# A decoder block's MLP down projection: the right-hand column blocks take three feature pairs as block products instead of two

## The chip, the cores and the metric

The kernel runs on one NeuronCore of a Trainium2 chip. The metric is the device time of one execution in microseconds (us). The engines are named as in the profile: PE does the matmuls (PEld its weight loads), DVE works on vectors, ACT evaluates activations and copies, POOL is little used, and SP's queue issues most of the DMAs.

## The reference, cut to what matters

The reference is one decoder block on 256 tokens of width 2048 in float32: an input projection, a gated convolution branch and an attention branch, a mixing product, a layer norm, a squared-ReLU MLP beside a gated per-layer embedding, and a second layer norm. The change touches the MLP's second product alone.

```python
h = jnp.square(jax.nn.relu(x @ w_mlp_up[i])) @ w_mlp_down[i]     # (256,2048) (2048,8192) -> (256,8192) (8192,2048) -> (256,2048)
ple = (p[i] @ w_ple[i]) * jax.nn.sigmoid(x @ w_ple_gate[i])
x = _layer_norm(DN_ALPHA * x + h + ple, ln2_g[i], ln2_b[i])
```

## The kernel before, in words

**Precision.** Every float32 operand is split into a rounded part `hi` and a remainder `lo` (`split`, L67; for streamed weights `wchunk`, L77: a DMA into `raw`, an ACT copy into `whi` at L86, a DVE subtraction into `wlo` at L88). One product is then three matmuls: high by high, low by high, high by low.

**Chunks.** The MLP runs in four chunks `c` of 2048 hidden features (L1078). In a chunk, eight `up` calls (L1045) compute 256 features each, into `h` with the features on the partitions; their results leave PSUM through the ACT copies into `ab` (L1051), a tile with tag `m2` that has two buffers. Then the chunk's part of the down projection is added to `y`, whose 2048 columns are four blocks of 512. Chunks 0 to 2 do this in the way described here; chunk 3 has a form of its own (L1172 on) that the change leaves alone.

**Two ways for a product.** The direct way is `xstat` (L131, lines 144, 145 and 148 of the trace): for each tile of 128 features and each half of the tokens three matmuls of 512 columns. The other way is class `Seven` (L638): two feature tiles (a pair), two token halves and two column blocks form a 2x2 by 2x2 block product that takes seven block products instead of eight. Sums of the activation blocks (`sums_to`, L629) and sums of the weight blocks are multiplied instead of the blocks themselves. For a pair `p` the steps are

- `load`: 1 MB of weights by SP's queue (L650) into `rs` or into the upper half of the tile `tr`;
- `b_forms`: split of two weight blocks (one ACT and one DVE instruction on 128x1024) into `forms` 8 to 11 or 12 to 15;
- `t_sums`: three DVE instructions (L659, L661, L662) that write four weight sums into `tf`, the lower half of `tr`;
- `t_forms`: their split (ACT and DVE on 128x2048) into `forms` 0 to 7;
- `products`: six of the products, three matmuls each (L685), numbered 1, 3, 5, 7, 6, 4, each into its own PSUM accumulator;
- `second`: the seventh product (L697), with weights streamed by `wchunk`.

`close` (L1097) adds the accumulators to four quarters of `y`: one ACT copy and ten DVE instructions (L1107), by way of three sums u2, u3 and u4.

**A chunk's down part.** The first two column blocks take all eight pairs as block products (`sv`), woven into the `up` calls: pair `p - 2`'s products stand ahead of steps of `up` call `p`. The third and the fourth block (`third`, L1126, and `fourth`, L1149) do twelve of their sixteen feature tiles directly, and pairs 6 and 7 as block products of a second object (`sv2`, L1124). `sv2` reuses the activation sums of `sv`, adds three of its products onto the direct blocks' accumulators (`onto`, L1147), and ends with a close of its own (L1169). Its order by hand stands in L1127 to L1169: the steps of `third` and `fourth`, the seventh products of `sv` (`more`), and between them the preparation of the pairs. PSUM bank 4 holds first `sv`'s seventh product and then `sv2`'s product 6. The next chunk's first `up` call writes banks 0 and 3, its second banks 1 and 2, later ones 0 and 1 (L1074).

**What sets the order.** The program is written as one sequence, and the framework makes each engine's own order from it ahead of the run with a planner that simulates the timeline (L1287). An instruction whose operands the planner thinks ready can go ahead of earlier ones on its engine; `after(...)` pins some behind others. On the chip each engine then runs its list in that order. A tile with a tag is a buffer that the next tile of the same tag takes over when all uses of the old one are done: `tr` (tag O), `forms` (tag C) and `h` (tag B) have one buffer, so a new chunk's `tr` begins when the last use of the old one has ended.

## Time and profile before

| what | value |
|---|---|
| median of 3 runs | 1806.29 us (1803.21 to 1806.33) |
| the profiled execution | 1808.8 us, its span 1807.0 us |
| mean granted TensorE clock | 0.996 |
| PE busy | 1791.2 us, 9259 matmuls |
| DVE busy | 1424.9 us |
| ACT busy | 1014.5 us |
| read from HBM | 363.33 MB |

Busy time of PE counts pipelined matmuls, so it says that PE had work, not that it was at its peak. Where the text speaks of a wait, the profile names the instruction that stood and the one whose end released it. The clock column gives the share of full speed that was granted to TensorE in a stretch.

### The profile page before, as it was taken

How to read it: one execution, taken by the hardware profiler on the slowest of the kernel's cores; microseconds unless marked ns; L12 is line 12 of the kernel's file. 1: busy time of each engine (PE TensorE's matmuls, PEld its weight loads, DVE VectorE, ACT ScalarE, POOL GpSimd, SP SyncE). 2: the span in 40 equal slices, each digit the busy share in tenths (PEclk: the TensorE clock that was granted, in tenths of full speed). 3: DMA queues.
4: the chain of work that ended last, by engine and by line, in shares of the span. 5: the costliest groups of instructions: out<-in, count | busy, mean ns of one | idle time of the engine just before them, and what ended most of it. 6: DMA issues, size and time to landing. Idle time of an engine off the chain costs nothing.

```text
span 1807.0 us, 24866 instructions
## 1 busy us (share of the span) xinstructions
PE 1791.2 (99%) x9259; PEld 1532.3 (85%) x9259; DVE 1424.9 (79%) x2033; ACT 1014.5 (56%) x1344; POOL 18.5 (1%) x33
## 2 busy tenths in 40 slices
PE   9999999999999999999999999999999999999998
PEld 7889888888888888888888888888888888888886
DVE  6776776767787987897698678888888888889765
ACT  5555555555555555555454745765666466647561
POOL 1000000000000000000000000000000000000010
PEclk9999999999999999999999999999999999999999
DMA  8777665566655755865674567665766667666572
GB/s 262 223 237 215 178 176 164 166 183 175 175 164 175 235 200 191 272 210 178 202 271 163 194 230 252 214 206 189 244 200 213 197 206 223 202 213 197 186 275 74
DMA packets 255032, 367.07 MB, mean 203 GB/s; under 512 B 10773, under 2 KB 175477, under 8 KB 254400
## 3 DMA queue, kind: packets, MB, share of 16 engines
q1 hardware_dynamic: 250128, 354.07, 61.8%
q0 software_dynamic: 2112, 8.81, 1.4%
q10 hardware_dynamic: 2672, 2.62, 0.5%
q8 instruction: 72, 1.18, 0.3%
q14 instruction: 48, 0.39, 0.1%
HBM read 363.33 MB, written 2.12 MB: 202 GB/s over the span
## 4 chain that ended last, share of the span: by engine, by line
PE 95%; DVE 2%; DMA 1%; ACT 1%; issue 1%; SPq 0%; DVEq 0%; ACTq 0%
PE mm L106 16%; PE s L106 13%; PE s L685 12%; PE s L144 10%; PE s L145 10%; PE s L148 10%; PE mm L112 8%; PE s L112 6%; PE s L697 2%; PE s L1224 1%; PE sc L500 1%; PE mm L144 1%; PE mm L145 1%; PE mm L148 1%; PE po L350 1%
## 5 line engine op out<-in xcount | busy, mean ns | idle before, releaser
L86 ACT ACTIVATE whi<-raw 128x1024 fp32r<-128x1024 f32 (+2 forms) x567 | 588.7, 1042 | 501.4 <-PE s L145 185.2
L88 DVE TENSOR_TENSOR wlo<-raw,whi 128x1024 fp32r<-128x1024 f32 (+2 forms) x567 | 675.6, 1199 | 211.7 <-issue 52.5
L106 PE MATMUL mm<-xT,whi 128*128 128x512 f32 x1280 | 313.5, 393 | 0.1
L106 PE MATMUL s<-x,whi 128*128 128x512 f32 x1024 | 268.9, 395 | 6.1 <-ACT ab L1051 6.1
L106 PEld LDWEIGHTS mm<-xT,whi 128*128 128x128 f32 x1280 | 234.0, 189 | 44.8 <-issue 0.6
L106 PEld LDWEIGHTS s<-x,whi 128*128 128x128 f32 x1024 | 185.9, 191 | 39.3 <-ACT ab L1051 6.7
L112 PE MATMUL mm<-xT,wlo 128*128 128x256 f32 x1280 | 181.5, 285 | 0.0
L112 PEld LDWEIGHTS mm<-xT,wlo 128*128 128x128 f32 x1280 | 169.9, 190 | 7.5
L112 PEld LDWEIGHTS s<-x,wlo 128*128 128x128 f32 x1024 | 142.7, 192 | 12.2 <-DVE wlo L88 1.0
L112 PE MATMUL s<-x,wlo 128*128 128x256 f32 x1024 | 146.9, 284 | 0.0
L69 DVE TENSOR_TENSOR forms<-tr,forms 128x2048 fp32r<-128x2048 f32 (+1 forms) x63 | 112.9, 1796 | 24.5 <-ACT forms L68 22.9
L68 ACT ACTIVATE forms<-tr 128x2048 fp32r<-128x2048 f32 (+1 forms) x63 | 95.1, 1515 | 20.3 <-PE s L685 6.3
L685 PE MATMUL s<-forms,sums 128*128 128x512 f32 x408 | 106.1, 390 | 0.0
L685 PEld LDWEIGHTS s<-forms,sums 128*128 128x128 f32 x408 | 76.3, 188 | 16.0
L145 PE MATMUL s<-whi,h 128*128 128x512 f32 x208 | 80.9, 389 | 0.0
L144 PE MATMUL s<-whi,h 128*128 128x512 f32 x208 | 80.4, 389 | 0.0
L1051 ACT ACTIVATE ab<-s 128x512 f32<-128x512 f32 x64 | 37.7, 597 | 49.5 <-PE s L106 46.7
L148 PE MATMUL s<-wlo,h 128*128 128x512 f32 x208 | 65.0, 390 | 0.4 <-DVE wlo L88 0.4
L685 PE MATMUL s<-forms,h 128*128 128x512 f32 x204 | 60.9, 391 | 0.0
L685 PE MATMUL s<-forms 128*128 128x512 f32 x240 | 60.3, 389 | 0.0
L685 PEld LDWEIGHTS s<-forms 128*128 128x128 f32 x240 | 45.0, 188 | 9.3
L69 DVE TENSOR_TENSOR forms<-t,forms 128x1024 fp32r<-128x1024 f32 x40 | 48.5, 1220 | 3.0 <-ACT forms L68 2.7
(337 smaller groups left out, 2775.3 us busy)
## 6 DMA issues: line engine op xcount, KB each, us to landing
raw<-in_w_in_dram SPq DMA_DIRECT2D x204, 512.0 KB, 4.2
raw<-in_w_mlp_up_dram SPq DMA_DIRECT2D x128, 512.0 KB, 4.5
raw<-in_w_mlp_down_dram SPq DMA_DIRECT2D x69, 512.0 KB, 3.6
rs<-in_w_mlp_down_dram SPq DMA_DIRECT2D x17, 1024.0 KB, 7.0
tr<-in_w_mlp_down_dram SPq DMA_DIRECT2D x17, 1024.0 KB, 6.8
raw<-in_w_conv_out_dram SPq DMA_DIRECT2D x32, 512.0 KB, 4.4
raw<-in_w_attn_out_dram SPq DMA_DIRECT2D x32, 512.0 KB, 4.3
raw<-in_w_ple_gate_dram SPq DMA_DIRECT2D x32, 512.0 KB, 4.1
```

Source lines behind the costliest of these rows:

```text
L68: last_hi[0] = nc.scalar.activation(hi, src, AF.Copy).ins
L69: last_lo[0] = nc.vector.tensor_sub(lo, src, f32(hi)).ins
L86: last_whi[0] = nc.scalar.activation(hi, raw, AF.Copy).ins
L88: last_wlo[0] = nc.vector.tensor_sub(lo, raw, f32(hi)).ins
L106: last_mm[0] = nc.tensor.matmul(ps[f].rearrange("p a t -> p (a t)"), hi[:, kk, f * P:(f + 1) * P], mov[:, k0 + kk].rearrange("p a t -> p ( ...
L112: last_mm[0] = nc.tensor.matmul(ps[f][:, 1, :], lo[:, kk, f * P:(f + 1) * P], mov[:, k0 + kk, 0, :], start=False, stop=False, skip_group_c ...
L144: nc.tensor.matmul(ps[t], sta[:, kt0 + kt, 0, ts], hi[:, kk, :], start=(kt == 0), stop=False)
L145: nc.tensor.matmul(ps[t], sta[:, kt0 + kt, 1, ts], hi[:, kk, :], start=False, stop=False)
L148: last_mm[0] = nc.tensor.matmul(ps[t], sta[:, kt0 + kt, 0, ts], lo[:, kk, :], start=False, stop=(kt == nkt - 1)).ins
L685: last_mm[0] = nc.tensor.matmul(self.acc[n], first[:, a, :], self.forms[:, w, :], start=(p == self.p0 and i == 0 and n not in self.onto), ...
L697: last_mm[0] = nc.tensor.matmul(ps, self.mat[:, 2 * (q + k) + 1, a, 0:P], w[:, k, :], start=(own is not None and q + k == 0 and i == 0), s ...
L1051: nc.scalar.activation(ab[:, f], ps[f], AF.Copy)
```

## The change

In chunks 0 to 2 the third and fourth block take pairs 5, 6 and 7 as block products and the first ten feature tiles directly.

- `third` and `fourth` run 10 tiles (five steps) instead of 12 (six steps).
- `sv2` starts at pair 5. It multiplies pair 6 first (`first`, which starts the accumulators), then 5, then 7. By the turns 6: 0, 5: 1, 7: 2 the loads go to `rs`, `tr`, `rs`, and the block splits to `forms` 8, 12, 8.
- Pair 5's activation sums must last to the chunk's end; they move to the buffer with tag `pT` (L1058).
- `second` handles an odd number of pairs: 5 and 6 together, then 7 alone.
- In `third`, all products of pair 7 of `sv` stand ahead of the fourth step, where they stood in two parts before the fifth step; the first close follows one step earlier.
- The second close keeps u2, u3 and u4 in `tf`, the weight sums' tile, and no longer in two `m2` buffers.

```diff
--- before.py
+++ after.py
@@ -642,7 +642,7 @@
         def __init__(self, rows, c0, mat, raw, t, forms, b, t0, n=8, p0=0):
             self.rows, self.c0, self.mat, self.raw, self.t, self.forms, self.b, self.t0, self.n, self.p0 = (
                 rows, c0, mat, raw, t, forms, b, t0, n, p0)
-            self.raws, self.ts, self.sums, self.acc, self.onto = {}, {}, {}, {}, {}
+            self.raws, self.ts, self.sums, self.acc, self.onto, self.first = {}, {}, {}, {}, {}, p0
 
         def load(self, p):
             self.raws[p] = self.raw(p)
@@ -676,14 +676,14 @@
                          self.sums[p][:, {5: 0, 7: 1, 6: 2, 3: 3}[n]])
                 hi = {1: b, 3: b + 1, 5: t0, 7: t0 + 1, 6: t0 + 2, 4: t0 + 3}[n]
                 lo = hi + (2 if n in (1, 3) else 4)
-                if p == self.p0:
+                if p == self.first:
                     if n in self.onto:
                         self.acc[n] = self.onto[n]
                     elif n not in self.acc:
                         self.acc[n] = bank({1: 2, 3: 3, 5: 4, 7: 5, 6: 6, 4: 7}[n])
                 for i, (a, w) in enumerate(((0, hi), (1, hi), (0, lo))):
                     last_mm[0] = nc.tensor.matmul(self.acc[n], first[:, a, :], self.forms[:, w, :],
-                                                  start=(p == self.p0 and i == 0 and n not in self.onto),
+                                                  start=(p == self.first and i == 0 and n not in self.onto),
                                                   stop=(p == self.n - 1 and i == 2),
                                                   skip_group_check=n in self.onto).ins
 
@@ -691,8 +691,9 @@
 
             for q in range(self.p0, self.n, 2):
                 ps = self.onto.get(2) or (self.acc[1] if own is None else own)
-                hi, lo = wchunk(self.rows[:, q:q + 2, 1, self.c0:self.c0 + 512], 2, 512)
-                for k in range(2):
+                nk = min(2, self.n - q)
+                hi, lo = wchunk(self.rows[:, q:q + nk, 1, self.c0:self.c0 + 512], nk, 512)
+                for k in range(nk):
                     for i, (a, w) in enumerate(((0, hi), (1, hi), (0, lo))):
                         last_mm[0] = nc.tensor.matmul(ps, self.mat[:, 2 * (q + k) + 1, a, 0:P], w[:, k, :],
                                                       start=(own is not None and q + k == 0 and i == 0),
@@ -1055,7 +1056,10 @@
         nc.scalar.activation(m, m, AF.Square)
         split(m, h[:, 2 * p:2 * p + 2, 0, :], h[:, 2 * p:2 * p + 2, 1, :])
         if p < sv.n:
-            sv.sums[p] = post.tile([P, 4, 2, P], F32R, tag="sg", name="sums")
+            if p == 5 and c < 3:
+                sv.sums[p] = post.tile([P, 4, 2, P], F32R, tag="pT", name="sums", bufs=1)
+            else:
+                sv.sums[p] = post.tile([P, 4, 2, P], F32R, tag="sg", name="sums")
             sums_to(m, sv.sums[p])
 
     def down(c, j, banks, nkt=KT):
@@ -1094,9 +1098,8 @@
         def quarters(c0):
             return [y[:, t, a:a + 512] for t in range(2) for a in (c0, c0 + 512)]
 
-        def close(a, y00, y01, y10, y11):
-            u = [post.tile([P, 2, 512], F32, tag="m2", name="u", bufs=2) for _ in range(2)]
-            u2, u3, u4 = u[0][:, 0], u[0][:, 1], u[1][:, 0]
+        def close(a, u, y00, y01, y10, y11):
+            u2, u3, u4 = u
             nc.scalar.activation(u2, a[1], AF.Copy)
             for out_, v, w, op in ((y00, y00, a[1], ALU.add), (y01, y01, a[3], ALU.add),
                                    (u2, u2, a[6], ALU.add), (u4, u2, a[5], ALU.subtract),
@@ -1121,52 +1124,58 @@
                     prep[i](p - 1)
             run(pair)
         sv.products(6, (1, 3, 5, 7, 6, 4))
-        sv2 = Seven(sv.rows, 1024, h, raw, sv.t, forms, sv.b, 0, p0=6)
+        turn_of = {6: 0, 5: 1, 7: 2}
+        sv2 = Seven(sv.rows, 1024, h, lambda p: raw(turn_of[p]), sv.t, forms, lambda p: 8 + turn_of[p] % 2 * 4, 0, p0=5)
+        sv2.first = 6
         left = [bank(0), bank(1)]
-        third = down(c, 2, left, 12)[0]
-        for i in range(6):
-            if i == 4:
-                sv.products(7, (5, 7, 6, 4))
+        third = down(c, 2, left, 10)[0]
+        for i in range(5):
+            if i == 3:
+                sv.products(7, (1, 3, 5, 7, 6, 4))
             next(third)
             if i < 3:
                 prep[i](7)
             if i == 0:
                 sv2.load(6)
             if i == 2:
-                sv.products(7, (1, 3))
-                sv2.load(7)
-            if i == 3:
+                sv2.load(5)
                 sv2.b_forms(6)
                 sv2.t_sums(6)
-            if i == 4:
-                close(acc, y00, y01, y10, y11)
+            if i == 3:
+                u = [post.tile([P, 2, 512], F32, tag="m2", name="u", bufs=2) for _ in range(2)]
+                close(acc, (u[0][:, 0], u[0][:, 1], u[1][:, 0]), y00, y01, y10, y11)
+                sv2.load(7)
         run(third)
         right = [bank(2), bank(3)]
         (n11, n21), (n12, n22) = left, right
         ps = bank(4)
         sv2.sums, sv2.onto = sv.sums, {2: n11, 3: n12, 4: n21}
         z00, z01, z10, z11 = quarters(1024)
-        fourth, more = down(c, 3, right, 12)[0], sv.second(ps)
-        for i in range(6):
+        fourth, more = down(c, 3, right, 10)[0], sv.second(ps)
+        for i in range(5):
             next(fourth)
             if i < 4:
                 next(more)
+            if i == 0:
+                sv2.t_forms(6)
             if i == 1:
-                sv2.t_forms(6)
-            if i == 2:
-                sv2.b_forms(7)
-                sv2.t_sums(7)
+                sv2.b_forms(5)
+                sv2.t_sums(5)
             if i == 3:
                 nc.vector.tensor_add(y00, y00, ps)
                 sv2.acc.update({1: bank(5), 5: bank(6), 7: bank(7), 6: bank(4)})
                 sv2.products(6, (1, 3, 5, 7, 6, 4))
-            if i == 4:
-                sv2.t_forms(7)
-        run(fourth, more, sv2.second(None))
+                sv2.t_forms(5)
+                sv2.b_forms(7)
+                sv2.t_sums(7)
+        run(fourth, more)
+        sv2.products(5, (1, 3, 5, 7, 6, 4))
+        sv2.t_forms(7)
+        run(sv2.second(None))
         for z, n in ((z11, n22), (z00, n11)):
             nc.vector.tensor_add(z, z, n)
         sv2.products(7, (1, 3, 5, 7, 6, 4))
-        close(sv2.acc, z00, z01, z10, z11)
+        close(sv2.acc, (tf[:, 0], tf[:, 1], tf[:, 2]), z00, z01, z10, z11)
 
 
     u2, u3, u4 = tf[:, 0], tf[:, 1], tf[:, 2]
```

## Prediction

> **What bounds the kernel now.** I read the page first, then PE's waits, the chain of waits around a chunk border, the granted clock there, and the orders of DVE, ACT and SP.

> ```profile
> PE 1791.2 (99%) x9259; PEld 1532.3 (85%) x9259; DVE 1424.9 (79%) x2033; ACT 1014.5 (56%) x1344; POOL 18.5 (1%) x33
> ```
> ```profile
> PE s L106 <- ACT ab L1051: 6.1, 3, 2.0
> ```

> PE is busy for 1791.2 of 1807.0 us, so time is won by fewer matmuls or by closing holes in PE. The waits of PE have one large row: three waits of 2.0 us, one at each chunk border. The chain at the first border:

> ```profile
> 1215.82 4.10 PE s L685 x18
> ...
> 1268.88 0.91 PE s L106 x4
> 1269.79 0.95 PE s L112 x8
> ...
> 1285.60 0.69 DVE forms L69
> 1286.29 0.61 DVE y L1107
> 1286.93 0.61 ACT ab L1051
> 1287.58 1.46 PE s L106 x4
> ```

> A 512-wide matmul takes 4.10/18 = 0.228 us, a 256-wide one 0.95/8 = 0.119. At 1287.58 PE restarts after a chain: a DVE weight-form split, then the second close's `y01 -= u4` (L1107), then ACT's copy of the first `up` block into `ab` (L1051), then PE, which needs that bank. The copy waits for DVE because `ab` shares the two `m2` buffers with the close's `u` tiles. The windows at the three borders (columns: length, PE, PEld, DVE, ACT and POOL busy, granted clock, DMA share, GB/s) show a second price:

> ```profile
> 1285.55:1287.58 2.03, 0.00 (x2) 0.00 (x1) 2.03 (x4) 0.93 (x3) 0.00 (x0) 1.00 0.00 0
> 1287.58:1290.50 2.92, 2.92 (x12) 2.48 (x13) 2.92 (x4) 0.43 (x1) 0.00 (x0) 0.63 0.19 45
> 1290.50:1294.90 4.40, 4.40 (x20) 3.62 (x19) 4.40 (x5) 1.59 (x3) 0.00 (x0) 0.86 0.91 278
> 1461.11:1463.95 2.84, 2.84 (x13) 2.40 (x13) 2.84 (x4) 0.43 (x1) 0.00 (x0) 0.73 0.16 32
> 1463.95:1468.50 4.55, 4.55 (x18) 3.67 (x18) 4.55 (x5) 0.85 (x1) 0.00 (x0) 0.79 0.84 260
> 1634.70:1637.40 2.70, 2.62 (x13) 2.18 (x14) 2.70 (x4) 0.52 (x2) 0.00 (x0) 0.83 0.12 31
> 1637.40:1642.30 4.90, 4.90 (x19) 3.90 (x19) 4.87 (x7) 1.73 (x3) 0.00 (x0) 0.75 0.89 260
> ```

> After each hole the granted clock falls for about 7 us. The time lost to it is length times the missing clock: 2.92 x 0.37 + 4.40 x 0.14 = 1.7 us, then 0.77 + 0.96 = 1.7, then 0.46 + 1.23 = 1.7. So a border costs 2.03 + 1.7 = 3.7 us, and the three 11.2 us.

> [...]

> **Part 1, the matmuls.** Per chunk the two direct blocks run 10 row tiles instead of 12: 2 x 2 x 6 = 24 matmuls go. Pair 5 comes back as six products of three (18) and a seventh in the `second` step (3). Net 3 fewer of 0.228 us in each of three chunks: 9 x 0.228 = 2.05 us saved, all on PE, the bound.

> **Part 2, what feeds them.** DVE's groups, in the fourth block (the first fence) and in the third (the second):

> ```profile
> L88 DVE TENSOR_TENSOR wlo<-raw,whi 128x1024 fp32r<-128x1024 f32 x11 | 13.4, 1222 | 5.5 <-issue 2.2 <-PE s L148 2.1 <-PE s L697 1.2
> L659 DVE TENSOR_TENSOR tr<-tr 128x1024 f32<-128x1024 f32 x1 | 1.2, 1215 | 0.0
> L661 DVE TENSOR_TENSOR tr<-tr 128x512 f32<-128x512 f32 x1 | 0.7, 681 | 0.0
> ```
> ```profile
> L69 DVE TENSOR_TENSOR forms<-tr,forms 128x2048 fp32r<-128x2048 f32 x2 | 4.6, 2282 | 0.0
> L1107 DVE TENSOR_TENSOR y<-y,s 128x512 f32<-128x512 f32 x4 | 2.7, 681 | 0.0
> L69 DVE TENSOR_TENSOR h<-ab,h 128x512 fp32r<-128x512 f32 x1 | 0.7, 683 | 0.0
> ```

> Removed per chunk: two `wlo` of 1.22 = 2.44 us. Added: pair 5's block split (as `wlo`, 1.22), its sums (1.22 + 2 x 0.68 = 2.58), the split of the sums (2.28) and half a `wlo` in `second` (bounded by the 128x512 split, 0.68): 6.76. DVE gains 4.3 us per chunk. ACT loses two `whi` and gains 1.5 us on the same shapes; at 56% it has room. The loads gain 0.25 MB per chunk (1 MB and 0.25 MB come, two of 0.5 MB go).

> Whether DVE's 4.3 us show is read from the stages third block, fourth block, border:

> ```profile
> 1219.90:1240.30 20.40, 20.40 (x92) 16.90 (x91) 19.76 (x25) 11.85 (x12) 0.00 (x0) 1.00 0.49 168
> 1240.30:1266.45 26.15, 26.15 (x117) 21.64 (x116) 17.78 (x18) 11.11 (x12) 0.00 (x0) 1.00 0.64 210
> 1266.45:1285.50 19.05, 19.05 (x103) 16.35 (x101) 18.41 (x20) 12.35 (x11) 0.00 (x0) 1.00 0.73 237
> ```

> The third block loses 12 matmuls (2.7 us) and one `wlo`: DVE then has 19.76 - 1.22 = 18.5 us for 17.7, and 0.8 spills over. The fourth has 26.15 - 17.78 = 8.4 us of DVE idle. It loses 12 matmuls and gains 21, so 9 x 0.228 = 2.05 us more room, against 0.8 + 4.3 + 1.22 = 6.3 us of new work: about 4.1 us stay free. So the addition lies beside PE, as far as its order allows. Bounds: nothing, if the idle takes it; 4.3 us per chunk, if it queues at the saturated border. I take nothing, nearest to the row with 8.4 us idle.

> Its order: pairs 6, 5 and 7 share the sums' tile `tf` and the forms 0 to 7, so after pair 6's last product comes a series: split of pair 5's sums, its products, pair 7's sums and their split, products, close. One split is

> ```profile
> 1267.33 1.92 ACT L68 ACTIVATE forms<-tr 128x2048 fp32r<-128x2048 f32 x1
> ```

> and DVE's 2.28: 4.2 us. PE covers the first with the fourth block's last step (12), pair 5's products 1 and 3 (6) and `second` (9): 27 x 0.228 = 6.2 us. It covers the next with pair 7's products 1 and 3 (1.4 us) and the next chunk's first `up` (32 wide and 32 narrow: 7.3 + 3.8 = 11.1 us), whose banks 0 and 3 only wait for two adds. Pair 7's sums (2.58 us of DVE) run behind pair 5's last 12 products (2.7 us). If that cover is gone, a split shows with up to 4.2 us.

> **Part 3, the second close in `tf`.** The first `ab` of the next chunk no longer shares a buffer with the close, so ACT can copy when the `up` block ends, and bank 0 is free for PE. But `tf` belongs to `tr`: nothing of the next chunk's `tr` starts until the close ends. Before, DVE ran ahead there:

> ```profile
> 1270.73 2.28 DVE L69 TENSOR_TENSOR forms<-tr,forms 128x2048 fp32r<-128x2048 f32 x1
> ...
> 1282.28 0.68 DVE L1107 TENSOR_TENSOR y<-y,s 128x512 f32<-128x512 f32 x1
> 1282.88 3.42 DVE L69 TENSOR_TENSOR forms<-tr,forms 128x1024 fp32r<-128x1024 f32 x2
> 1286.21 1.28 DVE L1107 TENSOR_TENSOR y<-y,u 128x512 f32<-128x512 f32 x2
> 1287.42 1.22 DVE L88 TENSOR_TENSOR wlo<-raw,whi 128x1024 fp32r<-128x1024 f32 x1
> ```
> ```profile
> 1281.67 4.16 ACT L86 ACTIVATE whi<-raw 128x1024 fp32r<-128x1024 f32 x4
> ```

> The 3.42 us at 1282.88 are the next chunk's forms, put before the close's last three sums and before a `wlo` whose `whi` ACT began at 1281.67. PE would have waited for that `wlo` until about 1288.6 too. With the close in `tf` those splits cannot be there: they need the new `tr`. So both reasons for the hole leave together. They are not needed until the third `up`, one block (11.1 us) later.

> New waits: ACT's copy of the first accumulator into u2 now follows the split's last read of `tf`; behind it on ACT stand `whi` of the next `up`, but PE's product 7 that the sums need comes later still, so nothing. SP's load of pair 1 into `tr`, and what is queued behind it, is the dearer one:

> ```profile
> 1273.04 0.37 SPq L650 DMA_DIRECT2D tr<-in_w_mlp_down_dram  x1
> 1277.12 13.64 SPq L81 DMA_DIRECT2D raw<-in_w_mlp_up_dram  x4
> ```

> It left at 1273.04, 0.03 us after the split's last read (1270.73 + 2.28 = 1273.01), and four `up` weights are queued behind it. It will follow the close's end instead, some 10 us later; an order that keeps it ahead of those weights would starve the second `up`. I count it at nothing, since the order on the queues is planned by readiness.

> The sum: 2.05 + 11.2 = 13.2 us. The profiled execution took 1808.8 us (span 1807.0), 2.5 over the median 1806.3; carried to the median, 1806.3 - 13.2 = 1793.1 us.

> **The rivals.**
> - *The hole stays.* PE waits at the same place for the `wlo` at 1287.42 or for a bank that the close frees late: the last read there, 1282.28 + 0.68 = 1282.96, leaves no room before the second `up` at about 1283. Then only the matmuls are won: 1804.2 us. For it speaks that DVE has no idle in the border's windows after 1285.55; against it, that the work ahead of that `wlo` is what the change moves.
> - *Half the price comes back*: the waits go and the clock still dips, or the holes shrink by that much: 2.05 + 6.1 = 8.2, 1798.1 us. [...]
> - *Slower, by DVE at the border.* Its 4.3 us do not fall into the fourth block's idle, since the series above puts pair 5's split and pair 7's block split, sums and split behind pair 6's last product, which waits for bank 4. The close ends late, the second `up`'s banks with it, and PE stands 4.3 us plus a clock dip of 1.7. That is 6.0 in place of 3.7, per chunk 2.3 - 0.68 = 1.6 us more: 3 x 1.6 = 4.8, 1811.1 us. It decides from a new loss of 3.7 + 0.68 = 4.4 us per chunk. For it: DVE is busy 18.41 of 19.05 us in the border window. Against it: 4.1 us that stay free in the fourth block.

> **How the numbers follow.** The forecast (hole gone) has 0.53, its own range 1790 to 1797; half the price 0.10; the hole stays 0.20; slower 0.17. 0.2% is 3.6 us, about what a measurement of this kernel can tell from no change. Faster than 1802.7: 0.53 + 0.10 = 0.63; within: 0.20; slower: 0.17. The range 1790 to 1808 holds the first three, but for 0.03 below it, and leaves the slower case out.

> **What would show it.** Right: nine fewer matmuls; no PE wait on L1051, the clock at 1.00 over the borders; `tr`'s load after the close's last subtraction; DVE idle in the fourth block down from 8.4 to about 4. Wrong: a PE wait of over 2 us on a `wlo`, a form or a bank in the fourth block or the next two `up` blocks, with a clock below 1.00 behind it; or matmuls saved and the waits on L1051 as long as before.

## The result, and the profile after

The changed kernel takes 1796.28 us in the median of 4 runs (1795.61 to 1797.42), the kernel before 1806.31 (1803.21 to 1807.23). The ratio is 0.9946, with a 95% interval of 0.993 to 0.9961: 10.0 us less, between 7 and 12.6. The forecast was 1793.1.

The first fence has PE's and DVE's totals of the changed kernel, the second PE's largest waits in the MLP (total, times, longest):

```profile
PE 1784.3 (99%) x9250; PEld 1525.7 (85%) x9250; DVE 1436.2 (80%) x2045; ACT 1015.5 (57%) x1347; POOL 18.5 (1%) x33
```
```profile
PE s L112 <- DVE wlo L88: 1.2, 3, 0.4
PE s L106 <- ACT ab L1052: 0.5, 1, 0.5
```

Nine matmuls are gone, and so are the three waits of 2.03 us on the copy into `ab` (now L1052). In their place stand three of 0.4 us on a `wlo` and one of 0.5. The stages of the first chunk, in the order third block, fourth block, border, with the same columns as in the prediction:

```profile
1218.33:1236.02 17.69, 17.69 (x80) 14.65 (x79) 17.01 (x21) 10.80 (x11) 0.00 (x0) 1.00 0.67 223
1236.02:1259.70 23.68, 23.68 (x106) 19.63 (x105) 18.89 (x21) 10.36 (x11) 0.00 (x0) 1.00 0.56 185
1259.70:1278.80 19.10, 19.10 (x101) 16.36 (x100) 15.93 (x15) 11.00 (x11) 0.00 (x0) 1.00 0.69 212
1278.80:1297.80 19.00, 18.60 (x104) 15.89 (x103) 17.67 (x25) 9.93 (x13) 0.00 (x0) 1.00 0.48 156
```

The second row ends with the direct steps, ahead of most of pair 5's products. With these, up to the next chunk's first `up`, the stage has about the 126 matmuls that the prediction reckons with (117 - 12 + 21):

```profile
1236.02:1263.89 27.87, 27.87 (x125) 23.08 (x123) 21.88 (x25) 13.02 (x13) 0.00 (x0) 1.00 0.58 186
```

DVE's idle in it is 27.87 - 21.88 = 6.0 us, where it was 8.4. The clock is 1.00 over the border, where it fell to 0.63 and 0.86 before. The new hole, first in the chain of waits, then in PE's order of time:

```profile
1286.83 1.40 PE s L106 x7
1288.22 1.14 DVE forms L69
1289.36 0.60 DVE y L1110
1289.96 1.15 DVE wlo L88
```
```profile
1290.14 0.61 PE L685 MATMUL s<-forms,sums 128*128 128x512 f32 x2
1291.15 0.74 PE L112 MATMUL s<-x,wlo 128*128 128x256 f32 x4 [0.40 <-DVE wlo L88]
```

A block split of the next chunk's pair 0 (L69) and one of the close's sums stand on DVE ahead of the `wlo` that PE needs.

To compare the MLP alone, take the first and the last start of the narrow `up` matmuls (L112), here before and after:

```profile
L112 PE MATMUL s<-x,wlo x1024: 274/283/442, 1103.7 to 1730.8; 128*128 128x256 f32 x171
```
```profile
L112 PE MATMUL s<-x,wlo x1024: 274/283/387, 1102.2 to 1719.1; 128*128 128x256 f32 x171
```

The stretch goes from 627.1 to 616.9 us, 10.2 less. The spans (1807.0 and 1794.4) differ by 12.6: the other 2.4 us lie ahead of the first `up` and behind the last, in work that is the same in both kernels.

### The profile page after: what moved, and what is told of

It reads as the page before. It is cut to its first block, busy times and chain, and to the rows that moved or that the text cites. A ratio compares the mean times of both kernels' runs of the same rounds, so it can differ in the third digit from the quotient of the medians.

```text
span 1794.4 us, 24828 instructions
## 1 busy us (share of the span) xinstructions
PE 1784.3 (99%) x9250; PEld 1525.7 (85%) x9250; DVE 1436.2 (80%) x2045; ACT 1015.5 (57%) x1347; POOL 18.5 (1%) x33
## 3 DMA queue, kind: packets, MB, share of 16 engines
q10 hardware_dynamic: 2672, 2.62, 0.5%
## 4 chain that ended last, share of the span: by engine, by line
PE 97%; DVE 1%; DMA 1%; issue 0%; ACT 0%; SPq 0%; DVEq 0%
PE mm L106 16%; PE s L685 12%; PE s L106 12%; PE s L144 10%; PE s L145 10%; PE s L148 10%; PE mm L112 9%; PE s L112 6%; PE s L698 2%; PE s L1233 1%; PE sc L500 1%; PE mm L144 1%; PE mm L145 1%; PE mm L148 1%; PE po L350 1%; PE po L572 1%
## 5 line engine op out<-in xcount | busy, mean ns | idle before, releaser
L86 ACT ACTIVATE whi<-raw 128x1024 fp32r<-128x1024 f32 (+2 forms) x564 | 584.2, 1039 | 457.4 <-PE s L145 168.7
L88 DVE TENSOR_TENSOR wlo<-raw,whi 128x1024 fp32r<-128x1024 f32 (+2 forms) x564 | 670.3, 1197 | 200.9 <-issue 50.3
L106 PE MATMUL mm<-xT,whi 128*128 128x512 f32 x1280 | 312.7, 393 | 0.1
L106 PEld LDWEIGHTS mm<-xT,whi 128*128 128x128 f32 x1280 | 233.4, 189 | 45.3 <-ACT whi L86 0.9
L106 PE MATMUL s<-x,whi 128*128 128x512 f32 x1024 | 267.6, 392 | 0.5 <-ACT ab L1052 0.5
L106 PEld LDWEIGHTS s<-x,whi 128*128 128x128 f32 x1024 | 183.9, 188 | 32.7 <-ACT ab L1052 0.7
L112 PE MATMUL mm<-xT,wlo 128*128 128x256 f32 x1280 | 181.5, 285 | 0.0
L112 PEld LDWEIGHTS mm<-xT,wlo 128*128 128x128 f32 x1280 | 169.9, 190 | 7.4
L112 PEld LDWEIGHTS s<-x,wlo 128*128 128x128 f32 x1024 | 143.5, 190 | 15.0 <-DVE wlo L88 2.5
L112 PE MATMUL s<-x,wlo 128*128 128x256 f32 x1024 | 147.9, 282 | 1.2 <-DVE wlo L88 1.2
L69 DVE TENSOR_TENSOR forms<-tr,forms 128x2048 fp32r<-128x2048 f32 (+1 forms) x66 | 120.1, 1819 | 27.6 <-ACT forms L68 27.2
L68 ACT ACTIVATE forms<-tr 128x2048 fp32r<-128x2048 f32 (+1 forms) x66 | 101.3, 1535 | 42.2 <-DMA tr<-in_w_mlp_down_dram 23.9
L685 PE MATMUL s<-forms,sums 128*128 128x512 f32 x444 | 121.4, 391 | 0.0
L685 PEld LDWEIGHTS s<-forms,sums 128*128 128x128 f32 x444 | 82.0, 188 | 16.7 <-DVE forms L69 0.4
L145 PE MATMUL s<-whi,h 128*128 128x512 f32 x184 | 71.6, 389 | 0.0
L144 PE MATMUL s<-whi,h 128*128 128x512 f32 x184 | 71.4, 389 | 0.0
L1052 ACT ACTIVATE ab<-s 128x512 f32<-128x512 f32 x64 | 37.7, 595 | 55.3 <-PE s L106 55.3
L685 PE MATMUL s<-forms,h 128*128 128x512 f32 x222 | 67.1, 390 | 0.0
L685 PE MATMUL s<-forms 128*128 128x512 f32 x240 | 60.3, 389 | 0.0
L148 PE MATMUL s<-wlo,h 128*128 128x512 f32 x184 | 59.1, 389 | 0.0
L685 PEld LDWEIGHTS s<-forms 128*128 128x128 f32 x240 | 45.0, 188 | 9.3
L69 DVE TENSOR_TENSOR forms<-t,forms 128x1024 fp32r<-128x1024 f32 x40 | 48.5, 1220 | 3.0 <-ACT forms L68 2.7
```

The costliest lines, as they stand in the source:

```text
L68: last_hi[0] = nc.scalar.activation(hi, src, AF.Copy).ins
L69: last_lo[0] = nc.vector.tensor_sub(lo, src, f32(hi)).ins
L86: last_whi[0] = nc.scalar.activation(hi, raw, AF.Copy).ins
L88: last_wlo[0] = nc.vector.tensor_sub(lo, raw, f32(hi)).ins
L106: last_mm[0] = nc.tensor.matmul(ps[f].rearrange("p a t -> p (a t)"), hi[:, kk, f * P:(f + 1) * P], mov[:, k0 + kk].rearrange("p a t -> p ( ...
L112: last_mm[0] = nc.tensor.matmul(ps[f][:, 1, :], lo[:, kk, f * P:(f + 1) * P], mov[:, k0 + kk, 0, :], start=False, stop=False, skip_group_c ...
```

## The experiments

Each "before" is the kernel before on the same chip. The stretch is the one just defined, in the profiled execution.

| kernel | median us | ratio to before, 95% | stretch us |
|---|---|---|---|
| tile move alone | 1797.41 | 0.9946 (0.9934 to 0.9959) | 616.6 |
| three pairs, sums in m2 | 1806.36 | 0.9998 (0.9989 to 1.0007) | 625.3 |
| sums in tiles of their own | 1805.12 | 0.9993 (0.9984 to 1.0002) | 624.1 |
| `tr` held to the close's end | 1798.62 | 0.9956 (0.9944 to 0.9969) | 619.1 |
| changed kernel again | 1797.13 | 0.9945 (0.9933 to 0.9958) | 615.8 |
| tile move again | 1796.90 | 0.9946 (0.9933 to 0.996) | 616.8 |
| order edge alone | 1795.21 | 0.9937 (0.9925 to 0.9949) | 615.1 |
| changed kernel, order edge | 1795.27 | 0.9936 (0.9924 to 0.9949) | 615.4 |
| changed kernel, DVE work twice | 1797.10 | 0.9949 (0.9935 to 0.9962) | 617.1 |
| three pairs in m2, order edge | 1799.64 | 0.9963 (0.995 to 0.9975) | 619.5 |

**Which part of the change makes the gain.** First the tile move alone, in the kernel before:

```diff
-        close(sv2.acc, z00, z01, z10, z11)
+        close(sv2.acc, z00, z01, z10, z11, (tf[:, 0], tf[:, 1], tf[:, 2]))
```

> The kernel before, two pairs as before, with only the second close's u2, u3 and u4 moved to the weight sums' tile. Theory (the hole at the chunk border is most of the gain, and this move alone closes it): 11.2 us less than before (three holes of 2.03 and three clock dips of 1.7), less what small new holes cost, so 9 to 11 us faster, matmuls unchanged at 9259, PE clock 1.00 at the borders. Rival (the gain needs the third pair, which shifts the border's work): about as before, the three waits on the copy into ab still there.

It is 9.0 us faster, with the ratio of the change itself. The other half, the third pair with the sums back in m2:

```diff
-        close(sv2.acc, (tf[:, 0], tf[:, 1], tf[:, 2]), z00, z01, z10, z11)
+        u = [post.tile([P, 2, 512], F32, tag="m2", name="u", bufs=2) for _ in range(2)]
+        close(sv2.acc, (u[0][:, 0], u[0][:, 1], u[1][:, 0]), z00, z01, z10, z11)
```

> The changed kernel with the second close's u2, u3 and u4 back in the two m2 buffers. Theory: the nine matmuls are won (2.05 us) and the holes come back, so 0 to 4 us faster than before, with waits of PE near 2 us at each border and a clock below 1.00 behind them. Rival (the third pair makes the gain): 9 to 11 us faster, no holes.

No gain: 1806.36 against 1806.41. The holes did not come back as one of 2 us, but as four smaller ones at each border, 7.9 us in all, and the clock did not fall behind them (0.999 in the mean of that execution), as it had been expected to:

```profile
PE s L685 <- ACT sums L68: 3.5, 3, 1.2
PE s L106 <- ACT ab L1052: 1.8, 3, 0.7
PE s L106 <- DVE y L1110: 1.6, 3, 0.7
...
PE s L112 <- DVE wlo L88: 1.0, 3, 0.4
```

So the gain is the tile move's.

**Why the tile move works.** The prediction named two reasons that leave together: `ab` shares m2 with the close's sums, and DVE's forms of the next chunk stand ahead of a `wlo`. Two kernels part them. In the first, the sums have tiles of their own, so that only the sharing goes:

```diff
-        close(sv2.acc, z00, z01, z10, z11)
+        ua = post.tile([P, 2, 512], F32, tag="pT", name="ua", bufs=1)
+        ub = post.tile([P, 512], F32, tag="ub", name="ub", bufs=1)
+        close(sv2.acc, z00, z01, z10, z11, (ua[:, 0], ua[:, 1], ub))
```

> The kernel before, with the second close's u2, u3 and u4 in tiles of their own, neither m2 nor the weight sums' tile: the first ab no longer shares a buffer, but the next chunk's tr still starts early. Theory A (the sharing of m2 alone makes the hole): the hole closes, 9 to 11 us faster. Theory B (DVE's early forms of the next chunk, ahead of a wlo that PE needs, make it): PE now waits for wlo instead of ab, a hole of about 2 to 3 us at each border stays, within 3 us of before.

```profile
1282.60 3.43 DVE L69 TENSOR_TENSOR forms<-tr,forms 128x1024 fp32r<-128x1024 f32 x2
1285.93 0.69 DVE L1109 TENSOR_TENSOR y<-y,ub 128x512 f32<-128x512 f32 x1
1286.54 0.69 DVE L1109 TENSOR_TENSOR y<-y,ua 128x512 f32<-128x512 f32 x1
1287.14 1.23 DVE L88 TENSOR_TENSOR wlo<-raw,whi 128x1024 fp32r<-128x1024 f32 x1
```
```profile
1286.37 1.20 PE L106 MATMUL s<-x,whi 128*128 128x512 f32 x4 [1.09 <-ACT whi L86]
1288.42 1.22 PE L112 MATMUL s<-x,wlo 128*128 128x256 f32 x8 [0.86 <-DVE wlo L88]
```

No wait on `ab` is left, and next to nothing is won: 1.3 us, inside its interval. PE now waits 0.86 us for that `wlo`, behind the same 3.4 us of forms on DVE. Ahead of it PE waits 1.09 us for a `whi`, which stands on ACT behind ACT's half of the same splits:

```profile
1278.70 2.87 ACT L68 ACTIVATE forms<-tr 128x1024 fp32r<-128x1024 f32 x2
...
1284.32 2.00 ACT L86 ACTIVATE whi<-raw 128x1024 fp32r<-128x1024 f32 x2
```

In the second kernel the sums stay in m2, and the early forms go, with the early load into `tr`, by a copy of one column that keeps `tr` in use to the end of the close:

```diff
-        close(sv2.acc, z00, z01, z10, z11)
+        with after(close(sv2.acc, z00, z01, z10, z11)):
+            nc.vector.tensor_copy(mv1[:, 0, 0:1], tf[:, 0, 0:1])
```

> The kernel before, u2, u3 and u4 still in m2, with one 128x1 DVE copy behind the second close that reads the weight sums' tile, so that the next chunk's tr cannot start until the close has ended. Theory A (sharing of m2 makes the hole): the copy into ab still waits for the close, the hole stays, within 3 us of before. Theory B (DVE's early forms): the close ends some 3 us sooner since the forms no longer stand ahead of its last sums, the wlo comes in time, the hole shrinks below 0.5 us, 8 to 11 us faster.

It is 7.8 us faster, although the sharing is still there. At the second and third border it keeps waits of 1.98 and 0.94 us on `ab`, where under 0.5 was expected. They are not the sharing's: this `ab` is that of the second `up`, and its copy stands on ACT behind a split that waits for the load into `tr`, which now comes late:

```profile
1462.71 1.06 ACT L68 ACTIVATE forms<-tr 128x1024 fp32r<-128x1024 f32 x1 [4.15 <-DMA tr<-in_w_mlp_down_dram]
...
1465.71 0.58 ACT L1051 ACTIVATE ab<-s 128x512 f32<-128x512 f32 x1
```

So with two pairs no run shows a cost of the sharing by itself, and Theory B holds. It is confirmed by an edit that changes neither a tile nor a load, and pins instructions on DVE alone:

```diff
                 with after(last_wlo[0]):
-                    nc.vector.tensor_tensor(out_, v, w, op=op)
+                    ended[0] = nc.vector.tensor_tensor(out_, v, w, op=op).ins
...
+        before_this = ended[0]
...
                 if p >= 1 and i < 3:
-                    prep[i](p - 1)
+                    with after(before_this if p < 3 else None):
+                        prep[i](p - 1)
```

(The loop of chunk 3 has the same edge.)

> The kernel before, all tiles as before (u in m2, the next chunk's loads into tr early), with only an order edge: DVE's preparation of the next chunk's pairs 0 and 1 is queued behind the close's last subtraction. Theory B (DVE's order alone makes the hole): 7 to 10 us faster, no hole above 1 us at a border on the wlo or ab. Rival (the early load into tr, or the sharing of m2, has a share): the hole shrinks by less than half, 0 to 4 us faster.

```profile
1278.76 1.28 DVE L1109 TENSOR_TENSOR u<-u,s 128x512 f32<-128x512 f32 x2
1279.95 0.68 DVE L1109 TENSOR_TENSOR y<-y,s 128x512 f32<-128x512 f32 x1
1280.55 1.29 DVE L1109 TENSOR_TENSOR y<-y,u 128x512 f32<-128x512 f32 x2
1281.75 1.22 DVE L88 TENSOR_TENSOR wlo<-raw,whi 128x1024 fp32r<-128x1024 f32 x1
1282.89 0.69 DVE L1109 TENSOR_TENSOR y<-y,u 128x512 f32<-128x512 f32 x1
1283.49 1.22 DVE L69 TENSOR_TENSOR forms<-rs,forms 128x1024 fp32r<-128x1024 f32 x1
```
```profile
L112 PE MATMUL s<-x,wlo x1024: 274/283/287, 1103.1 to 1718.2; 128*128 128x256 f32 x171
```

The close's sums are now parted only by that `wlo`, which starts at 1281.75 where it started at 1287.42, and the profile lists no wait of PE in the stretch. It is 11.4 us faster, above the 7 to 10 expected, with two pairs and the sums in m2. On the same chip the change itself wins 9.5; the two intervals overlap.

The planner made ACT's order anew as well. Of the two splits that stood ahead of four `whi` on ACT, the longer one went behind them (the first line is from the kernel before, the second from this one):

```profile
1278.90 2.87 ACT L68 ACTIVATE forms<-tr 128x1024 fp32r<-128x1024 f32 x2
```
```profile
1297.35 1.90 ACT L68 ACTIVATE forms<-tr 128x2048 fp32r<-128x2048 f32 x1
```

So what is shown is the cost of the next chunk's splits being early, on DVE and on ACT together; no run parts the two engines' shares. In the kernel before, the profile names DVE.

**What the third pair is worth.** The changed kernel and the tile move alone, once more on one chip, without an edit:

> The changed kernel itself, once more, beside the next one on the same chip. What is asked is what the third pair is worth. By the sum: nine matmuls (2.05 us) less the new small holes (1.7 us of PE waits against 0.8 with the tile move alone), so about 1.1 us below the tile move alone; if the third pair is worth its nine matmuls in full, 2.05 below.

> The kernel before with the tile move alone, once more, on the same chip as the changed kernel: 8.5 to 10 us faster than before, and about 1.1 us above the changed kernel (0 if the third pair is worth nothing).

1797.13 and 1796.90: no difference. With the order edge on the changed kernel (the same edit as above):

> The changed kernel with the same order edge. In it PE still waits 0.4 us three times for a wlo that stands behind the block split of the next chunk's pair 0. Theory B: these three holes close, 0.5 to 1.5 us below the changed kernel. Rival (those holes come from wlo being late for other reasons): as the changed kernel.

1795.27, against 1795.21 for the same edge with two pairs. The holes on `wlo` closed, and the median is 1.9 us under the changed kernel, but one wait of 0.8 us on a form's split came at the last border. Twice, then, the nine matmuls (2.05 us) are not seen in the time.

The profiled executions show where most of them went. From start to start PE needs 0.228 us (`up`) or 0.227 (down) for a 512-wide matmul and 0.120 for a narrow one; what goes beyond that by over 0.015 us, summed over the stretch, is its loss. It is 3.1 us in the changed kernel and 1.5 with the tile move, and 1.6 with the order edge on three pairs against none with two. So three pairs lost 1.6 us of the 2.05 to new gaps each time. In the repeat on one chip the losses were 2.1 and 1.7, and the stretch was 1.0 us shorter with three pairs, which the medians do not show; at intervals of over 2 us to either side the rest stays open. And the order edge on three pairs with m2:

> The changed kernel with u2, u3 and u4 back in m2 and the order edge instead of the tile move: three pairs, DVE's preparation of the next chunk behind the close. Theory B (order alone counts, the m2 buffers do not): near the changed kernel or up to 2 us below, holes of 0 to 1 us per border. Rival (with three pairs the close ends later, so that m2 is now what PE waits for): holes of 1 to 2 us at each border, 3 to 8 us above the changed kernel.

```profile
PE s L112 <- DVE wlo L88: 2.1, 6, 0.5
...
PE s L106 <- DVE y L1112: 1.4, 3, 0.5
```

1799.64 is between the two theories. With three pairs the close comes later, and order alone leaves 3.5 us of waits; with the tile move beside it (1795.27, on another chip) the time was some 4 us less.

**Whether DVE's added work binds.** The changed kernel with pair 5's preparation done twice:

```diff
-                sv2.b_forms(5)
-                sv2.t_sums(5)
+                for _ in range(2):
+                    sv2.b_forms(5)
+                    sv2.t_sums(5)
```

> The changed kernel with pair 5's block split and sums of the weights done twice, to the same values, in the fourth block: DVE gets 1.22 + 2.58 = 3.8 us more per chunk in the place where the prediction counted 4.1 us of idle left. Theory (that idle takes it): within 1.5 us of the changed kernel. Rival of the prediction (DVE is the bound around the border, what it gets more PE waits for): 3.8 us and perhaps a clock dip at each border, 8 to 16 us slower than the changed kernel.

1797.10 against 1797.13: another 3.8 us of DVE work per chunk (DVE's busy total rose from 1436.2 to 1445.7 us) costs nothing there. The amount of work is not what binds; its place in the order is.

**How often the clock falls behind a hole.** Two kernels put fifteen holes into the kernel of the order edge, with one turn or three in each. PE's later matmuls are queued behind the last tiny one:

```diff
+    def hole(turns):
+        pb = bank(0)
+        with after(last_mm[0]):
+            last_mm[0] = nc.tensor.matmul(pb[:, 0:16], ident, ident[:, 0:16], start=True, stop=True).ins
+        for _ in range(turns):
+            v = post.tile([P, 16], F32, tag="v", name="v", bufs=1)
+            nc.scalar.activation(v, pb[:, 0:16], AF.Copy)
+            last_mm[0] = nc.tensor.matmul(pb[:, 0:16], ident, v, start=True, stop=True).ins
+        return last_mm[0]
...
+            turned = hole(TURNS) if p >= 3 else None
```

> The kernel of the order edge (which has no hole in the MLP) with fifteen holes put into PE, ahead of up calls 3 to 7 of three chunks: a tiny matmul, an ACT copy of 16 columns, a tiny matmul that needs it, and the rest of PE queued behind. One turn, a hole of some 0.7 to 1.2 us. [...] By the holes seen so far (2.03 us dips, 0.4 us does not): few or no dips.

> The same with three turns, a hole of some 2 to 3.2 us with two tiny matmuls in it, fifteen times. [...]

Each ran once: 1832.72 us with one turn, 1872.39 with three. Of the kernel with one turn, a hole, the stretch at half clock behind it, a second hole, and the time behind that one:

```profile
1138.40:1139.90 1.50, 0.03 (x1) 0.03 (x1) 1.50 (x2) 1.42 (x3) 0.00 (x0) 1.00 0.25 74
1141.07:1144.48 3.41, 3.41 (x11) 2.76 (x11) 2.79 (x4) 2.59 (x4) 0.00 (x0) 0.50 0.76 217
1157.30:1158.90 1.60, 0.02 (x2) 0.00 (x1) 1.60 (x2) 1.55 (x3) 0.00 (x0) 1.00 0.49 108
1160.00:1164.00 4.00, 4.00 (x25) 3.50 (x24) 3.29 (x6) 2.72 (x5) 0.00 (x0) 1.00 0.81 220
```
```profile
PE s L1085 <- ACT v L1084: 21.9, 15, 1.6
```

Fifteen holes of 21.9/15 = 1.46 us gave four dips; the three-turn kernel's fifteen, with 34.6/15 = 2.3 us of waits each, gave thirteen.

## Why the prediction was right, and where its sizes were off

- **The hole at the border: right.** The three waits on L1051 and the dips behind them are gone, the clock is 1.00. The reason was half right. The sharing of m2, which the chain of waits named, was not the binding one: without it next to nothing was won. The early forms, ahead of the close's last sums and of a `wlo`, were; the order edge alone showed it, with the part of ACT said above.
- **Part 1, the matmuls: right in number, not in worth.** 9250 for 9259; but with two pairs the kernel is as fast, by either way of closing the hole. The median fell by 10.0 us, less than the 11.2 of the holes alone, so this term is not what brought the forecast near.
- **Part 2, "I take nothing": the term that was mis-sized.** The room was there (6.0 us of idle for the 4.1 worked out, and twice the work costs nothing), and the split series was covered. But the order left new holes, 1.2 + 0.5 = 1.7 us of waits. In starts they cost more: the two matmuls at 1290.14 need 0.45 us, the next starts at 1291.15, so 0.56 us are lost where 0.40 are booked as idle. Over the stretch, PE's loss from start to start was 11.9 us before (the prediction had 11.2 for it) and 3.1 after: 11.9 + 2.05 - 3.1 = 10.9 us were due, and 10.2 came.
- **The load on SP: right in its place, not quite nothing in its price.** It left right after the close's last subtraction:

```profile
1291.01 0.69 DVE L1110 TENSOR_TENSOR y<-y,tr 128x512 f32<-128x512 f32 x1
```
```profile
1291.73 0.37 SPq L650 DMA_DIRECT2D tr<-in_w_mlp_down_dram  x1
```

  PE was not starved by it at the borders. But the wait of 0.5 us on `ab`, at 1665.80, comes from a load into `tr`: ACT stood 4.51 us for it, with that copy behind. The kernel with `tr` held, where such waits are 3.2 us in all, shows how dear a late load can be.

- **The carrying over to the median.** The sum went by an execution with all three dips, 2.5 us above the median. Dips vary from run to run: the mean granted clock of the runs of before lies between 0.996 and 0.998, 0.996 in the profiled one, and three dips of 1.7 us are 0.003 of the span. So an average run had less to win. The 39 runs of before beside the experiments bear this out: the 20 at 0.996 took 1807.0 us in the mean, the 16 at 0.997 1805.9, the 3 at 0.998 1804.7. How much of the shortfall this makes is not tried.
- **The rivals.** Slower by DVE: the doubled work speaks against it. The hole stays: this is what three pairs without the tile move do. Half the price: its time, 1798.1, is nearer to the median than the forecast (1.8 us above it, against 3.2 below), but its reasons are not what happened: the clock did not dip any more (1.00 at all three borders), and the holes shrank by more, from 11.9 to 3.1 us in starts. The new small holes took part of the difference, the variation of the dips perhaps the rest.

## What to carry to other kernels

The wait that the profile names is the one that ended last; a second one can stand right behind it (here 0.86 us on a `wlo`, once the wait on `ab` was gone), so ask what the waiting engine would have met next before a buffer is added. On an engine that works through a list in order, look for long instructions that nobody waits for yet ahead of short ones that the bound engine needs (here 3.42 us of splits ahead of a `wlo` of 1.22): an order edge needs no work and no memory, and here won at least as much as the change (11.4 us against 9.5). To hold a buffer back does the same and delays its next load, which an engine that works in order passes on to all that stands behind (ACT stood 4.15 us for it, and PE 1.98 us for the copy behind). A saving of 0.1% in matmuls (2.05 us) is not worth a longer series at a border unless the holes beside it are counted too (here 1.6 us more).

## What the runs showed of the hardware

In the kernel before, each of the three dips is 3.41 us at half clock:

```profile
1288.33:1291.74 3.41, 3.41 (x13) 2.86 (x13) 3.41 (x5) 0.00 (x0) 0.00 (x0) 0.50 0.50 152
1462.40:1465.81 3.41, 3.41 (x13) 3.02 (x13) 3.41 (x4) 0.00 (x0) 0.00 (x0) 0.50 0.61 166
1636.48:1639.89 3.41, 3.41 (x13) 2.83 (x12) 3.41 (x4) 0.00 (x0) 0.00 (x0) 0.50 0.66 172
```

```profile
1464.36:1466.34 1.98, 0.00 (x1) 0.00 (x0) 1.98 (x3) 1.98 (x4) 0.00 (x0) 1.00 0.15 52
1466.34:1474.00 7.66, 7.66 (x41) 6.66 (x42) 7.66 (x10) 7.16 (x9) 0.00 (x0) 1.00 0.86 279
```

The length of a hole does not part them. In the kernel before, the 3.413 us ahead of each dip hold 2.03, 2.03 and 1.71 us of PE's idle time. In the one-turn kernel the clock falls at 1141.07, behind the hole of 1.50 us up to 1139.90, while behind the one of 1.60 us at 1157.30 it stays at 1.00. By what rule the clock falls, these runs do not show.
